# A hybrid encoder trunk on one core: the builder resumes its chains by an account of queues and tiles instead of by fixed times

## The chip, the core and the metric

The kernel runs on one core of one Trainium2 chip. The core has five engines with a queue of instructions each: TensorE (PE, matrix products; its weight loads are shown as PEld), VectorE (DVE), ScalarE (ACT), GpSimd (POOL) and SyncE (SP, which issues the DMAs). An engine takes its instructions in the order in which they stand in its queue and waits, where it must, on semaphores. The metric is the time of one execution on the device, in microseconds (us).

## The reference, cut to what matters

Two groups of tokens (512 of "prompt", 256 of "sample") go through the same two layers. They share the weights and nothing else.

```python
def swiglu(h, w_in, w_out):
    gate, up = jnp.split(h @ w_in, 2, axis=-1)
    return (jax.nn.silu(gate) * up) @ w_out

def mixer(h, lp, rope):
    z = h @ lp["w_mix_in"]
    xb, yb, zr, q, k, v = jnp.split(z, [...], axis=-1)
    o_lru = rglru_mixer(xb, yb, lp)          # conv, gates, scan in both directions
    o_rwkv = rwkv_mixer(zr, lp)              # 4 heads of 64, delta rule, both directions
    o_att = attention(q, k, v, ...)          # 6 heads, 2 of them for keys and values
    return jnp.concatenate([o_lru, o_rwkv, o_att], axis=-1) @ lp["w_mix_out"]

def layer(x, c, lp, rope):
    sh1, sc1, g1, ... = jnp.split(silu(c) @ lp["w_ada"] + lp["b_ada"], 9)
    h = rmsnorm(x, g[0]) * (1 + sc1) + sh1
    x = x + 0.5 * g1 * swiglu(h, ffn_w_in[0], ffn_w_out[0])
    h = rmsnorm(x, g[1]) * (1 + sc2) + sh2
    x = x + g2 * mixer(h, lp, rope)
    h = rmsnorm(x, g[2]) * (1 + sc3) + sh3
    return x + 0.5 * g3 * swiglu(h, ffn_w_in[1], ffn_w_out[1])
```

D_MODEL is 1024, D_FF 2816, DEPTH 2; all of it in float32.

## The kernel before

All activations are held transposed: features on the 128 partitions, tokens along the free axis. PS is the prompt sequence (512 columns), SS the sample sequence (256 columns).

**Dense products.** A float32 weight is loaded (`wr`), rounded to fp32r by ACT (`wh`, L270), and the rest is formed by DVE (`wl`, L271). An activation is split in the same way (`xn`, `an`, `xo`, each a pair). One product of a 128x128 block is three matmuls: wh by xh, wh by xl, wl by xh. The PSUM tiles name the stage: `pg`, `pu` (PS) and `pb` (SS) for the feed-forward input, `ops` for the feed-forward output and the mixer's output, `mip` for the mixer's input. These are 15,264 of the 21,882 matmuls. DVE and ACT have one `wl` and one `wh` to make for each 512 columns of weights; for SS, such a piece serves 12 matmuls of 256 columns, for PS 12 of 512.

**Chains.** Between them run small products that wait on each other through DVE, ACT and POOL. The rwkv chain of a pair of heads (`rwkv_pair`) is the longest: `up`/`ap` (gates), a scan on DVE (`cu`), `kkp` (norm of the key), `bp` (bonus), then `AR`, `csum`, `BK`, `aa` and `B` on DVE, POOL and ACT (L763 to L806), then `scps` (scores), `btps`, `vtps`, four levels of `yps`/`dps` (a triangular inverse), the loop `zps`/`saps`/`stps` over chunks, `ywp` (output), a group norm on DVE that ends in `yy` (L1011), `yp`, `gp`. It runs twice a layer for each sequence. Behind the second pair comes the mixer's output product, `ops<-xo`, whose inputs `xo` are split from tiles that were spilled (`ol`) and from `yy`. A norm is `ssp` (sum of squares), a reciprocal root in some 12 tiny DVE instructions, and eight pairs `xn` by DVE, ACT and every third by POOL.

**What sets the order.** PE's queue is written in exactly the order in which the builder emits (L1187, `manual_schedule`); the other engines are ordered by the framework's scheduler, which goes by the order of emission, with the weights' `wh` and `wl` put ahead (L268). The builder is a small planner (L57 to L100): threads are generators, `Sched.t` is the planned time of PE, and each matmul adds its cost to it. A thread that yields a number may go on when that much planned time has passed; the numbers are the table `LAT` (L44), one per step and sequence. PS and SS are "dense" threads; attention, lru and the rwkv pairs are spawned as small threads. When PS is in its chains, SS supplies dense work, and the other way round: the small threads go first unless PE's debt to the dense ones exceeds `SLACK`.

```python
LAT = {... 'CH': (0.96, 0.58), 'NRM': (3.0, 3.0), 'XO': (1.7, 4.0), 'PREP': (5.0, 8.2), ... 'R8': (8.64, 6.0)}
            th.ready = self.t + r        # a thread that yielded r
```

So the distance between two steps of a chain, counted in dense matmuls that stand between them in PE's queue, comes from this table alone.

Of the kernel before, what the change touches and what calls it, by code (L numbers as in the profile page):

```python
# [51 lines left out]
NR = 4  # L52

# [7 lines left out]
class Sched:  # L61
# [21 lines left out]

    def run(self):
        while self.threads:
            act = [th for th in self.threads if th.cond is None or th.cond()]
            assert act, "stuck"
            now = [th for th in act if th.ready <= self.t + 1e-9]
            if not now:
                self.t = min(th.ready for th in act)  # L90
                continue
            dn = sorted((th for th in now if th.dense), key=lambda h: (h.prio() if callable(h.prio) else h.prio, h.ready))
            sn = sorted((th for th in now if not th.dense), key=lambda h: (h.prio() if callable(h.prio) else h.prio, h.ready))
            t0 = self.t
            if sn and (self.debt <= SLACK or not dn):
                self.step(sn[0])
                self.debt += (self.t - t0) * self.ratio
            else:
                self.step(dn[0])
                self.debt = max(0.0, self.debt - (self.t - t0))  # L100

# [10 lines left out]
def trunk_kernel(ctx, tc, xT, cT, wadh, wada, wfi, wfo, wmi, wmo, prm, gatew, loraw, cst, rope, scanm, outT, dbg=None):  # L112
    nc = tc.nc
    V, A, G, PE = nc.vector, nc.scalar, nc.gpsimd, nc.tensor
    sch = Sched(RATIO)

# [13 lines left out]
    def dbank(n=512, name="db"):  # L130
        return psd.tile([128, n], F32, name=name, tag="d")

    def sbank(n=512, name="sb"):
        return pss.tile([128, n], F32, name=name, tag="m")
# [11 lines left out]

    def mm(out, lhsT, rhs, start=True, stop=True, cost=None):
        PE.matmul(out, lhsT, rhs, start=start, stop=stop, skip_group_check=True)  # L148
        k, m, n = lhsT.shape[0], lhsT.shape[-1], rhs.shape[-1]
        if cost is not None:  # L150
            sch.t += cost
        elif rhs.dtype == F32R:
            sch.t += (n / 2.4 if n >= 256 else 213) * 1e-3
        else:
            conc = 1.0
            if m <= 32:
                conc = 4.0
            elif m <= 64:
                conc = 2.0
            sch.t += max(4 * max(n, m) / 2.4 / conc, 33.0) * 1e-3  # L160

    def trp(out, src, idn, cost=0.11):
        PE.transpose(out, src, idn)
        sch.t += cost
# [47 lines left out]
    def ada_load(src):  # L212
        u = adap.tile([128, 1024], F32, name="adaw", tag="adaw")
        nc.sync.dma_start(out=u, in_=src)
        return [u[:, j * 256:j * 256 + 256] for j in range(4)]
# [21 lines left out]
    def ada(l, m, lat):  # L237
        ps = sbank(256, name="adaps")
        for k in range(KD):
            for j, u in enumerate(ada_load(wada[l * 9 + m, k])):  # L240
                mm(ps[32 * j:32 * j + 32, :], sc[:, k, :], u, start=(k == 0), stop=(k == KD - 1))
            if k % ADQ == ADQ - 1:
                yield lat
# [20 lines left out]
    def wtile(dt, name):  # L264
        return wsp.tile([128, 512], dt, name=name, tag=name)
# [30 lines left out]
    def weight_raw(u):  # L296
        raw = wsp.tile([128, 1024], F32, name="wr", tag="wr", bufs=NR)
        nc.sync.dma_start(out=raw[:, :u.shape[-1]], in_=u)
        return raw
# [85 lines left out]
    class Norm:  # L385
# [19 lines left out]
        def apply(self):  # L405
            q, l, i = self.q, self.l, self.i
            self.x = []
            for k in range(KD):
# [11 lines left out]
                yield LAT["CH"][q.i] if k < KD - 1 else LAT["NRM"][q.i]  # L420
# [99 lines left out]
    def mix_in(q, l, xs, M):  # L520
# [3 lines left out]
        nc.sync.dma_start(out=rp, in_=rope[:, :, 0:n])  # L524
# [70 lines left out]
    def attention(q, l, M):  # L595
        n, nt = q.n, q.nt
        yield lambda: M.stage >= 1
        yield LAT["A0"][q.i]
# [22 lines left out]
        yield LAT["A1"][q.i]  # L621
# [3 lines left out]
        def stA(u):  # L625
# [3 lines left out]
            mm(S, M.qs[j][b0:b0 + 64, c0:c0 + 128], kr[b0:b0 + 64, :])  # L629
# [22 lines left out]
        def stC(u):  # L652
# [6 lines left out]
            for kt in range(nt):  # L659
                mm(o[b0:b0 + 64, :], vt[:, kt * 128 + b0:kt * 128 + b0 + 64], PT[:, kt * 128:kt * 128 + 128],  # L660
                   start=(kt == 0), stop=(kt == nt - 1))
# [13 lines left out]
    def lru(q, l, M):  # L675
        p, d_, n = pr[l], prm_d[l], q.n
        yield lambda: M.stage >= 2
        yield LAT["L0"][q.i]
# [44 lines left out]
    def rwkv_pair(q, l, hp, M):  # L723
# [95 lines left out]
        for d in range(2):  # L819
            for h in range(2):  # L820
                SC[h][d] = c128(slot(q, "SC"))
            for c0 in range(0, nch, 4):
                pp = [sbank(512, name="scps") for h in range(2)]
                for c in range(4):
                    for h in range(2):
                        b = 64 * h
                        mm(pp[h][:, c * 128:c * 128 + 128], bk(h, d * nch + c0 + c), AR[d][b:b + 64, :, (c0 + c) * 64:(c0 + c) * 64 + 64],
                           cost=0.11)
# [13 lines left out]
        for e in range(nbk):  # L842
            pp = [sbank(wb, name="btps") for h in range(2)]
            for c in range(gpb):
                for h in range(2):
                    trp(ch(pp[h], c), bk(h, e * gpb + c), ident[64 * h:64 * h + 64, 64 * h:64 * h + 64], 0.03)
# [97 lines left out]
        for i in range(nch):  # L944
            gs = (i, NC2 - 1 - i)
            sel = slice(i, NC2 - i, NC2 - 1 - 2 * i)
            if i > 0:
                zp = sbank(128, name="zps")
                for d, g in enumerate(gs):
                    for b in (0, 64):  # L950
                        mm(zp[b:b + 64, d * 64:d * 64 + 64], ar(b, g, 0), S0[b:b + 64, g, :])
# [13 lines left out]
            for d, g in enumerate(gs):  # L965
                for h in range(2):
                    mm(dp[64 * h:64 * h + 64, d * 64:d * 64 + 64], ch(BT[h], g), ch(SAV[h], g))
# [66 lines left out]
    def layer_thread(q, th):  # L1034
# [5 lines left out]
        if not P0:  # L1040
            prio(-2)
            yield S0T
            for k in range(KD):
                nc.sync.dma_start(out=q.x[k], in_=xT[k][:, q.o:q.o + q.n])
# [8 lines left out]
        for l in range(DEPTH):  # L1053
# [45 lines left out]
            for k in range(4):  # L1099
                nc.sync.dma_start(out=q.xd[k], in_=q.xsp[l][k])  # L1100
# [178 lines left out]
```

## Time and profile before

| | |
|---|---|
| time, median of 3 runs | 3456.47 us (3454.62 to 3456.97) |
| the profiled execution | 3462.16 us, of which the span from first to last instruction 3459.2 us |
| mean granted clock of TensorE | 0.986 of full speed |
| busy share of the span | PE 97%, PEld 79%, DVE 58%, ACT 42%, POOL 15% |
| DMA queue of the loads | 441 MB, 40% of the 16 engines' span |

A busy PE is not a PE at its peak: matmuls overlap, so the distance from start to start is shorter than the duration shown, and a matmul at half clock counts as busy too. The stretches named later are: 674 to 1046 us and 2193 to 2524 us, where PS is in its rwkv chains and SS does dense work (layers 0 and 1); 1046 to 1184 us, where PS begins its second feed-forward; 2524 to 2816 us, the same in layer 1; 1184 to 1586 us, where SS is in its rwkv chains and PS does dense work.

### The profile page before, as it was taken

What the parts mean: (1) busy time and instruction counts of PE and PEld (TensorE: products, weight loads), DVE (VectorE), ACT (ScalarE), POOL (GpSimd) and SP (SyncE); (2) the same over time, 40 slices, a digit from 0 to 9 for tenths busy, and PEclk for the clock granted to TensorE, in tenths of its full rate; (3) what the DMA queues carried; (4) which work ended last, traced back from release to release, by engine and by line L of the source; (5) the groups of instructions that cost most, each with busy time, mean ns of one, the idle gap of its engine ahead of it and who ended that gap; (6) DMA issues with size and microseconds to landing.
All of it is one profiled execution on the core that took longest, in us unless ns stands there. A gap on an engine that the chain in (4) does not pass through costs nothing. (4 is left out here: it accounts for less than half of the span.)

```text
span 3459.2 us, 69173 instructions
## 1 busy us (share of the span) xinstructions
PE 3341.5 (97%) x28052; PEld 2734.0 (79%) x28052; DVE 2003.2 (58%) x3973; ACT 1448.2 (42%) x2730; POOL 512.1 (15%) x659
## 2 busy tenths in 40 slices
PE   7999999999899899999999999999899999999999
PEld 5777776678877777888888876788789978778899
DVE  4433365775776745546333476667557776446466
ACT  3322243644346433434333346534345564334354
POOL 1100020212221211111000111212211111111010
PEclk9999999999999999999999999999899999999999
DMA  7666674133342222423332331233245533223455
GB/s 276 219 206 208 203 270 145 57 104 113 100 153 93 83 80 83 132 90 119 92 98 86 119 114 62 79 110 102 82 161 164 179 106 108 63 91 125 138 177 161
DMA packets 151630, 445.80 MB, mean 129 GB/s; under 512 B 16912, under 2 KB 20752, under 8 KB 151312
## 3 DMA queue, kind: packets, MB, share of 16 engines
q1 hardware_dynamic: 151312, 441.39, 40.2%
q8 instruction: 220, 3.60, 0.4%
q14 instruction: 98, 0.80, 0.1%
HBM read 427.17 MB, written 14.16 MB: 128 GB/s over the span
## 5 line engine op out<-in xcount | busy, mean ns | idle before, releaser
L270 ACT ACTIVATE wh<-wr 128x512 fp32r<-128x512 f32 (+1 forms) x1368 | 816.6, 602 | 1572.1 <-PE ops L148 485.5
L271 DVE TENSOR_TENSOR wl<-wr,wh 128x512 fp32r<-128x512 f32 (+1 forms) x1368 | 907.3, 668 | 800.4 <-ACT wh L270 769.8
L148 PE MATMUL ops<-an,wh 128*128 128x512 f32 (+1 forms) x2816 | 717.8, 345 | 19.3 <-ACT an L351 7.3
L148 PEld LDWEIGHTS ops<-an,wh 128*128 128x128 f32 x2816 | 480.1, 190 | 99.1 <-issue 13.5
L148 PE MATMUL pb<-xn,wh 128*128 128x256 f32 x2816 | 525.1, 287 | 0.5 <-issue 0.5
L148 PE MATMUL ops<-an,wl 128*128 128x512 f32 (+1 forms) x1408 | 477.2, 339 | 0.1
L148 PE MATMUL pg<-xn,wh 128*128 128x512 f32 x1408 | 449.5, 400 | 7.8 <-ACT xn L417 5.9
L148 PEld LDWEIGHTS pb<-xn,wh 128*128 128x128 f32 x2816 | 433.6, 189 | 19.2 <-issue 11.2
L148 PE MATMUL pu<-xn,wh 128*128 128x512 f32 x1408 | 447.4, 399 | 0.0
L352 POOL TENSOR_TENSOR an<-sg,an 128x512 fp32r<-128x512 f32 (+1 forms) x176 | 192.3, 1093 | 1674.0 <-ACT an L351 1613.0
L148 PE MATMUL pb<-xn,wl 128*128 128x256 f32 x1408 | 396.4, 282 | 4.8 <-DVE wl L271 3.8
L431 DVE SCALAR_TENSOR_TENSOR x<-ops,gat,x 128x256 f32<-128x256 f32 (+1 forms) x352 | 215.8, 614 | 196.0 <-PE ops L148 190.6
L148 PE MATMUL mip<-xn,wh 128*128 128x512 f32 (+1 forms) x1216 | 314.2, 348 | 9.3 <-DVE f L583 2.9
L148 PEld LDWEIGHTS pg<-xn,wh 128*128 128x128 f32 x1408 | 260.1, 188 | 75.6 <-ACT xn L417 6.5
L148 PEld LDWEIGHTS pu<-xn,wh 128*128 128x128 f32 x1408 | 260.1, 188 | 65.5 <-issue 6.6
L148 PEld LDWEIGHTS ops<-an,wl 128*128 128x128 f32 x1408 | 267.0, 190 | 31.6 <-DVE wl L271 0.3
L148 PE MATMUL pg<-xn,wl 128*128 128x512 f32 x704 | 277.4, 394 | 0.0
L148 PE MATMUL pu<-xn,wl 128*128 128x512 f32 x704 | 276.8, 393 | 0.0
L148 PEld LDWEIGHTS pb<-xn,wl 128*128 128x128 f32 x1408 | 265.9, 189 | 6.0 <-DVE wl L271 4.8
L148 PEld LDWEIGHTS mip<-xn,wh 128*128 128x128 f32 x1216 | 208.2, 192 | 48.9 <-issue 12.3
L148 PE MATMUL mip<-xn,wl 128*128 128x512 f32 (+1 forms) x608 | 207.2, 341 | 0.0
L148 PEld LDWEIGHTS pg<-xn,wl 128*128 128x128 f32 x704 | 132.9, 189 | 30.7
(257 smaller groups left out, 3738.5 us busy)
## 6 DMA issues: line engine op xcount, KB each, us to landing
wr<-in_wfi_dram SPq DMA_DIRECT2D x352, 512.0 KB, 3.6
adaw<-in_wada_dram SPq DMA_DIRECT2D x128, 512.0 KB, 4.4
wr<-in_wfo_dram SPq DMA_DIRECT2D x192, 256.0 KB, 2.7
wr<-in_wfo_dram SPq DMA_DIRECT2D x128, 320.0 KB, 2.9
wr<-in_wmi_dram SPq DMA_DIRECT2D x76, 512.0 KB, 3.6
wr<-in_wmo_dram SPq DMA_DIRECT2D x32, 512.0 KB, 3.5
adaw<-in_wadh_dram SPq DMA_DIRECT2D x32, 256.0 KB, 5.2
xsp<-x SPq DMA_DIRECT2D x8, 512.0 KB, 3.6
```

What stands on the lines that cost most here:

```text
L148: PE.matmul(out, lhsT, rhs, start=start, stop=stop, skip_group_check=True)
L270: A.activation(out=hi[:, :n], in_=raw, func=AF.Copy)
L271: V.tensor_tensor(out=lo[:, :n], in0=raw, in1=hi[:, :n].bitcast(F32), op=ALU.subtract)
L352: eng.tensor_tensor(out=lo, in0=src, in1=hi.bitcast(F32), op=ALU.subtract)
L431: V.scalar_tensor_tensor(out=q.x[m], in0=ps, scalar=gat[l][:, i, m, q.i:q.i + 1], in1=q.x[m], op0=ALU.mult, op1=ALU.add)
```

## The change

An account (`Model`) is kept beside the planner. `Engine` wraps VectorE, ScalarE and GpSimd: each instruction still goes out as before, and the account books it on a list of busy intervals of that engine, in the first gap that is long enough from the moment on at which its inputs are ready, whether or not something later was already booked. Durations are linear in the size, with constants for kinds of instruction. For each tile the account keeps when it is written (`w`), read for the last time (`r`) and, for tiles that are taken through `alloc` (PSUM, weights, adaLN weights), when its buffer comes free (`free`). A tile of the slot pools isn't taken through `alloc`, so its `free` is 0, and a load into it (`load`) is booked as there at `DMAT` = 3.4 us from the start of the program. That an instruction writes a tile which an earlier one still reads isn't booked.

With it, a step resumes as follows. A chain that yields a positive `LAT` resumes 0.05 us after the last of the instructions that its step issued (`step_last`), so the numbers in `LAT` act as a flag; a yield of 0.0 is as before. Dense steps yield `At(...)`, the time at which the account has their weights and the next two activation pairs ready. Norms and the split of `xo` yield `At(step_last - 1.6)`. A small thread also waits until the account has one of the four PSUM buffers free. Planned costs of matmuls are raised (0.4531 ns a column for fp32r instead of 0.4167), and a change between dense and small matmuls costs 0.1 us in the plan. Instructions of every kind are as many as before: PE 21,882 matmuls, DVE 3,967 rows, ACT 2,660, POOL 664, SP 1,051.

```diff
+SWITCH = 0.1
+DMAT = 3.4
...
     def step(self, th):
+        self.mo.step_last = 0.0
...
+        elif isinstance(r, At):
+            th.ready = r.t
+        elif r > 0 and self.mo.step_last > 0:
+            th.ready = self.mo.step_last + 0.05
         else:
             th.ready = self.t + r
...
-            now = [th for th in act if th.ready <= self.t + 1e-9]
+            bank = self.mo.bank("m")
+            now = [th for th in act if max(th.ready, 0.0 if th.dense else bank) <= self.t + 1e-9]
...
+    def place(self, t0, dur):
+        iv = self.iv
+        k = len(iv)
+        while k > 0 and iv[k - 1][1] > t0:
+            k -= 1
+        s = t0
+        while k < len(iv) and iv[k][0] < s + dur:
+            s = max(s, iv[k][1])
+            k += 1
+        iv.insert(k, (s, s + dur))
...
+    def op(self, e, name, outs, ins, kw):
...
+        t0 = self.ready(*ins)
+        for a in outs:
+            t0 = max(t0, self.free.get(self.keys(a)[0][0], 0.0))
...
+        t = e.place(t0 + 0.06, d) + lag
+        for a in outs:
+            for k in self.keys(a):
+                self.w[k] = max(self.w.get(k, 0.0), t) if name != "memset" else max(self.w.get(k, 0.0), t)
...
+        self.step_last = max(self.step_last, t)
...
+    def dma(self, out, src):
+        t = max(self.free.get(self.keys(out)[0][0], 0.0), self.ready(src) if hasattr(src, "tensor") else 0.0)
+        for k in self.keys(out):
+            self.w[k] = t + DMAT
...
     def mm3(out, q, xs, every):
         nk = len(xs)
         for k, (xh, xl) in enumerate(xs):
             if k % 4 == 0:
+                wfill(q, look(q) + 1)
+                yield At(mo.ready(*q.wq[0], *xs[k], *xs[min(k + 1, nk - 1)]) if k else
+                         max(mo.ready(*q.wq[0], *xs[0], *xs[min(1, nk - 1)]), mo.free.get(out.tensor.name if hasattr(out, "tensor") else out.name, 0.0)))
                 wh, wl = wget(q)
+            elif k % every == 0:
+                yield At(mo.ready(*xs[k], *xs[min(k + 1, nk - 1)]))
...
-            if k % every == every - 1:
-                yield 0.0
...
                 self.x.append((xh, xl))
-                yield LAT["CH"][q.i] if k < KD - 1 else LAT["NRM"][q.i]
+                yield At(mo.step_last - 1.6)
...
             for k in range(3):
                 od.append(slot(q, "ol"))
-                nc.sync.dma_start(out=od[k], in_=q.osp[l][k])
+                load(od[k], q.osp[l][k])
             for t in [od[k // 2][:, k % 2, :] for k in range(6)] + M.orw:
                 xh, xl = pair(q, "xo")
                 split(xh, xl, t)
                 xo.append((xh, xl))
-                yield LAT["CH"][q.i]
+                yield At(mo.step_last - 1.6)
             M = None
             n3 = Norm(q, l, 2)
-            yield LAT["XO"][q.i]
             yield from out_proj(q, l, 1, xo, n3, EV[q.i])
```

Three places show what this does to the order. The first is PE's queue in SS's first rwkv pair of layer 0, from `kkp` to the first `scps`. Before:

```order
L148 MATMUL kkp<-ksq,cs 128x256
L148 MATMUL pu<-xn,wh 128x512 x2
L148 MATMUL pu<-xn,wl 128x512
...
L148 MATMUL bp<-kb,cs 128x256
L148 MATMUL pu<-xn,wh 128x512 x2
...
L148 MATMUL scps<-AR,BK 128x128
```

And now, in the same place:

```order
L309 MATMUL kkp<-ksq,cs 128x256
L309 MATMUL pu<-xn,wh 128x512 x2
L309 MATMUL pu<-xn,wl 128x512
...
L309 MATMUL bp<-kb,cs 128x256
L309 MATMUL pg<-xn,wh 128x512 x2
...
L309 MATMUL scps<-AR,BK 128x128
```

Before, 6 dense matmuls of 512 columns stand between `kkp` and `bp` and 96 between `bp` and `scps`, 102 in all. Now they are 24 and 18, 42 in all.

The second is PE's queue at the end of PS's second rwkv pair of layer 0, from the last output products `ywp` to the mixer's output product `ops<-xo`. Before:

```order
L148 MATMUL ywp<-S_10243,AR 64x64 x28
L148 MATMUL mip<-xn,wh 128x256 x2
...
L148 MATMUL yp<-cs,yy 64x64 x16
L148 MATMUL gp<-f,lw 128x512
L148 MATMUL mip<-xn,wh 128x256 x2
...
L148 MATMUL ops<-xo,wh 128x512 x2
L148 MATMUL ops<-xo,wl 128x512
```

And now:

```order
L309 MATMUL ywp<-S_10179,AR 64x64 x28
L309 MATMUL ssp<-acc,cs 128x256
L309 MATMUL yp<-cs,yy 64x64 x16
L309 MATMUL gp<-f,lw 128x512
L309 MATMUL ops<-xo,wh 128x512 x2
L309 MATMUL ops<-xo,wl 128x512
```

Before, 48 matmuls of SS stand between `ywp` and `yp` and 114 between `gp` and `ops<-xo`. Now there is one small `ssp` in the first gap and nothing in the second.

The third is DVE's queue behind the same `gp`, where `yy<-yy,gp` closes the pair and the eight low parts `xo` follow. Before:

```order
L1022 TENSOR_TENSOR yy<-yy,gp 128x512
L271 TENSOR_TENSOR wl<-wr,wh 128x512 x2
L352 TENSOR_TENSOR xo<-ol,xo 128x512 x2
L534 TENSOR_SCALAR qg<-mip,pr_99 128x256
L352 TENSOR_TENSOR xo<-ol,xo 128x512 x2
...
L352 TENSOR_TENSOR xo<-yy,xo 128x512 x2
```

And now:

```order
L128 TENSOR_TENSOR yy<-yy,gp 128x512
L128 SCALAR_TENSOR_TENSOR nx<-x_111,scl_132,rB 128x256
L128 SCALAR_TENSOR_TENSOR nx<-x_112,scl_132,rB 128x256
L128 TENSOR_TENSOR xo<-ol,xo 128x512 x2
L128 SCALAR_TENSOR_TENSOR xn<-nx,mod_130,xn 128x256 x2
L128 TENSOR_TENSOR xo<-ol,xo 128x512 x4
L128 TENSOR_TENSOR xo<-yy,xo 128x512
L128 TENSOR_TENSOR wl<-wr,wh 128x512
L128 TENSOR_TENSOR xo<-yy,xo 128x512
```

The eight splits now stand closer together, with five instructions of other work among them and ahead of them; they still stand behind `yy<-yy,gp`. (All wrapped instructions now carry line 128.)

## Rows read from the trace of the kernel before

**Rows 1.** The page: its first line.
```profile
span 3459.2 us, 69173 instructions
```

**Rows 2.** Windows: length; busy (instructions) of PE, PEld, DVE, ACT, POOL; clock; DMA; GB/s.
```profile
674.00:1046.00 372.00, 342.30 (x5092) 301.71 (x5091) 252.79 (x538) 156.09 (x308) 78.60 (x106) 0.96 0.37 114
1046.00:1184.00 138.00, 126.19 (x682) 98.74 (x681) 96.44 (x208) 83.65 (x171) 31.58 (x51) 0.95 0.30 95
1184.00:1586.00 402.00, 401.23 (x3284) 321.07 (x3284) 203.57 (x408) 139.69 (x264) 54.17 (x67) 1.00 0.31 95
2193.00:2524.00 331.00, 301.13 (x4799) 265.12 (x4799) 207.10 (x432) 136.13 (x268) 70.72 (x95) 0.94 0.31 94
2524.00:2816.00 292.00, 285.11 (x2083) 265.11 (x2082) 210.04 (x426) 157.32 (x301) 41.24 (x53) 0.99 0.53 168
```

**Rows 3.** Waits of PE: who waited for whom, us in total, times, longest.
```profile
PE scps L148 <- DVE BK L793: 13.8, 3, 6.1
...
PE pg L148 <- ACT xn L417: 5.9, 2, 5.5
...
PE yp L148 <- DVE yy L1011: 3.5, 3, 1.2
...
PE S L148 <- DVE qr L613: 2.3, 2, 1.4
```

**Rows 4.** Timeline of PE, PS's first rwkv pair: start, length, instruction, count [idle before].
```profile
710.67 0.40 PE L148 MATMUL ops<-an,wh 128*128 128x256 f32 x2
...
711.03 1.02 PE L148 MATMUL kkp<-ksq,cs 128*128 128x512 f32 x2
...
739.38 0.79 PE L148 MATMUL scps<-AR,BK 64*128 64x128 f32 x2 [6.06 <-DVE BK L793]
```

**Rows 5.** Timelines of DVE and ACT, the same pair: the last inputs of scps.
```profile
738.64 1.28 DVE L793 TENSOR_TENSOR BK<-aa,cu 128x512 f32<-128x512 f32 x2
...
739.36 2.00 ACT L806 ACTIVATE B<-BK 64x1024 f32<-64x1024 f32 x2 [4.24 <-DVE BK L793]
```

**Rows 6.** Timeline of PE, SS's first rwkv pair of layer 0.
```profile
1162.11 0.62 PE L148 MATMUL pu<-xn,wh 128*128 128x512 f32 x2
...
1162.80 0.59 PE L148 MATMUL kkp<-ksq,cs 128*128 128x256 f32 x2
...
1187.06 0.40 PE L148 MATMUL pu<-xn,wl 128*128 128x512 f32 x1
1187.38 0.37 PE L148 MATMUL scps<-AR,BK 64*128 64x128 f32 x1
```

**Rows 7.** Timelines of DVE and ACT, the same pair: the last inputs of scps.
```profile
1175.60 0.76 DVE L793 TENSOR_TENSOR BK<-aa,cu 128x256 f32<-128x256 f32 x2 [0.59 <-POOL aa L790]
...
1176.06 0.63 ACT L806 ACTIVATE B<-BK 64x512 f32<-64x512 f32 x1 [2.97 <-DVE BK L793]
```

**Rows 8.** Timeline of PE, end of PS's second rwkv pair of layer 0.
```profile
997.86 1.85 PE L148 MATMUL ywp<-S,AR 64*64 64x64 f32 x56
...
1013.55 1.15 PE L148 MATMUL yp<-cs,yy 64*64 64x64 f32 x32 [1.16 <-DVE yy L1011]
1014.63 1.12 PE L148 MATMUL gp<-f,lw 128*128 128x512 f32 x2
...
1029.01 0.64 PE L148 MATMUL ops<-xo,wh 128*128 128x512 f32 x2
```

**Rows 9.** Timeline of DVE, the same place.
```profile
1012.72 0.69 DVE L1011 TENSOR_TENSOR yy<-yy,rs 128x512 f32<-128x512 f32 x1
...
1019.77 1.29 DVE L352 TENSOR_TENSOR xo<-ol,xo 128x512 fp32r<-128x512 f32 x2
...
1028.90 1.28 DVE L352 TENSOR_TENSOR xo<-yy,xo 128x512 fp32r<-128x512 f32 x2
```

**Rows 10.** Timeline of PE: first use of PS's norm, layer 0.
```profile
1135.93 0.79 PE L148 MATMUL pg<-xn,wh 128*128 128x512 f32 x1 [5.45 <-ACT xn L417]
```

**Rows 11.** Windows around that wait (columns as in rows 2).
```profile
1133.00:1148.00 15.00, 8.73 (x34) 7.21 (x35) 14.89 (x21) 8.60 (x15) 5.83 (x13) 0.54 0.13 44
```

More of the change, by code (lines that the diff above doesn't have):

```diff
@@ L52, with __init__ @@
 NR = 4
+SWITCH = 0.1
+DMAT = 3.4
+class At:
+    def __init__(self, t):
+        self.t = t
 class Thread:
@@ L87, in run @@
             assert act, "stuck"
-            now = [th for th in act if th.ready <= self.t + 1e-9]
+            bank = self.mo.bank("m")
+            now = [th for th in act if max(th.ready, 0.0 if th.dense else bank) <= self.t + 1e-9]
             if not now:
-                self.t = min(th.ready for th in act)
+                self.t = min(max(th.ready, 0.0 if th.dense else bank) for th in act)
                 continue
@@ L100, in run, with __init__, __getattr__ @@
                 self.debt = max(0.0, self.debt - (self.t - t0))
+class Engine:
+    def __init__(self, real, m, kind):
+        self.real, self.m, self.kind, self.iv = real, m, kind, []
+    def __getattr__(self, name):
+        call = getattr(self.real, name)
+        def run(*args, **kw):
+            r = call(*args, **kw)
+            aps = [a for a in args if hasattr(a, "dtype") and hasattr(a, "shape")]
+            outs = [kw[k] for k in ("out", "accum_out") if kw.get(k) is not None]
+            ins = [v for k, v in kw.items() if k not in ("out", "accum_out") and hasattr(v, "dtype") and hasattr(v, "shape")]
+            if "out" not in kw:
+                outs, aps = outs + aps[:1], aps[1:]
+            self.m.op(self, name, outs, ins + aps, kw)
+            return r
+        return run
+    def place(self, t0, dur):
[8 more added lines that the diff above has]
+        iv.insert(k, (s, s + dur))
+        if len(iv) > 400:
+            del iv[:200]
+        return s + dur
@@ L149, in mm @@
         k, m, n = lhsT.shape[0], lhsT.shape[-1], rhs.shape[-1]
[L150 to L160, printed above, removed]
+        old = cost if cost is not None else (n / 2.4 if n >= 256 else 213) * 1e-3 if rhs.dtype == F32R else max(
+            4 * max(n, m) / 2.4 / (4 if m <= 32 else 2 if m <= 64 else 1), 33.0) * 1e-3
+        if cost is None:
+            if rhs.dtype == F32R:
+                cost = (n * 0.4531 if n >= 256 else 213) * 1e-3
+            else:
+                conc = 1.0
+                if m <= 32:
+                    conc = 4.0
+                elif m <= 64:
+                    conc = 2.0
+                cost = max(4 * max(n, m) * 0.4453 / conc, 33.0) * 1e-3
+        mo.mm(out, (lhsT, rhs), cost, old)
     def trp(out, src, idn, cost=0.11):
         PE.transpose(out, src, idn)
-        sch.t += cost
+        mo.mm(out, (src, idn), cost, cost)
     cs = const.tile([128, NCST], F32, name="cs")
@@ L597, in attention @@
         yield lambda: M.stage >= 1
-        yield LAT["A0"][q.i]
+        yield At(mo.ready(*M.sq))
         rps = sbank(3 * nt * 2, name="rqps")
@@ L620, in attention @@
         M.sq = M.vf = None
-        yield LAT["A1"][q.i]
+        yield At(mo.ready(kr, vt, *M.qs[0:3]))
         units = [(j, qt, hh) for j in range(3) for qt in range(nt) for hh in range(2)]
@@ L628, in stA @@
             S = sbank(n, name="S")
-            mm(S, M.qs[j][b0:b0 + 64, c0:c0 + 128], kr[b0:b0 + 64, :])
+            mm(S, M.qs[j][b0:b0 + 64, c0:c0 + 128], kr[b0:b0 + 64, :], cost=n * 2.1e-3)
             mx = tn(1, name="mx")
@@ L660, in stC @@
                 mm(o[b0:b0 + 64, :], vt[:, kt * 128 + b0:kt * 128 + b0 + 64], PT[:, kt * 128:kt * 128 + 128],
-                   start=(kt == 0), stop=(kt == nt - 1))
+                   start=(kt == 0), stop=(kt == nt - 1), cost=0.25)
             if hh == 1:
@@ L677, in lru @@
         yield lambda: M.stage >= 2
-        yield LAT["L0"][q.i]
+        yield At(mo.ready(*M.xc))
         M.ol = []
```

116 lines of the change are left out of this document (100 added, 16 removed).

## The prediction

> **What bounds the kernel now.** I read the page first, then the windows by stage, then PE's waits, and then the timelines around the waits that the change moves. The page gives a span of 3459.2 us [rows 1]; the profiled execution took 3462.16 us, 3.0 more, and 5.7 more than the median of the runs (3456.47). My sum is made on 3462.16, and 5.7 comes off at its end. PE is busy for 97% of the span, no other engine for more than 58%, so PE's queue is the bound, and only two things can be won or lost: time in which PE waits, and time in which it runs at half clock behind a wait.
>
> The windows show where these lie [rows 2]. While SS is in its chains (1184 to 1586 us) PE idles 402.00 - 401.23 = 0.8 us at clock 1.00: the order of before hides these chains entirely, and nothing is to be won there. While PS is in its chains PE idles 372.00 - 342.30 = 29.7 us at clock 0.96, and 29.9 us at 0.94 in layer 1. At the start of PS's second feed-forward (1046 to 1184) it idles 11.8 us at 0.95, in layer 1 (2524 to 2816) 6.9 us at 0.99. The half clock does not come by itself: in the 15 us around PE's wait of 5.45 us for `xn` [rows 10] the granted clock is 0.54 [rows 11], so 6.9 us of work are lost there besides the wait.
>
> Among PE's waits, `scps` for `BK` is 13.8 us in three, `pg` for `xn` 5.9, `yp` for `yy` 3.5, the attention's `S` for `qr` 2.3 [rows 3]. The question for each step is how long it takes on DVE, ACT and POOL, and how many dense matmuls stand beside it on PE. A dense matmul counts for its distance from the next start. With 256 columns three take 711.03 - 710.67 = 0.36 us, 0.12 each [rows 4]; with 512 columns 1162.80 - 1162.11 = 0.69, 0.23 each [rows 6].
>
> **SS, kkp to scps.** Before, 102 dense matmuls cover this step, 23.7 us; the rows agree (1162.80 to 1187.38) [rows 6]. It needs less: `kkp` ends at 1163.39, the last `B` is ready at 1176.69, 13.3 us later [rows 6, 7]. Of the 42 matmuls that now stand there (36 in the fourth pair) 9.7 us of cover are left (8.4), with `bp` 10.1 (8.8). So `scps` comes 3.2 us late in three pairs and 4.5 in one, 14 in all. The 13.3 us hold some dense work of DVE that the shorter step carries less of, so I take +12. Bounds: 0, if the chain shrinks with its cover, and 26, if each wait is followed by as much loss in clock as in rows 11. Matmuls taken from here stand elsewhere in the queue, where, by rows 2, nothing waits for them.
>
> **PS, kkp to scps.** Here `BK` already comes late: `kkp` starts at 711.03, `BK` ends at 739.92, PE waits 6.06 us [rows 4, 5]. From `lr` to `scps` the four pairs lose 3, 30, 15 and 30 matmuls of cover, 78 x 0.118 = 9.2 us. DVE is busy for 253 of the stretch's 372 us [rows 2] and the amount of other work in this part of its queue is nearly the same, so a good part of that shows as wait: +5 (0 to 9).
>
> **PS, ywp to yp.** The group norm takes 13.7 us from the end of `ywp` (999.71) to the last `yy` (1013.41) [rows 8, 9], and `yp` still waits 1.16 us behind its 48 matmuls in that pair. Over the four pairs the cover falls from 318 to 183 matmuls, by 16 us, to none in the second pair. Part of the 13.7 us is DVE doing other work, of which there is less now: +5 (0 to 16).
>
> **The split of xo.** Before, the first `xo` is ready at about 1020.4, 4.7 us after `gp` (1015.75), the last at 1030.18, 14.4 after it [rows 8, 9]; 114 matmuls, 13.4 us, lie between, and `ops` starts at 1029.01 with no wait. Now nothing lies between in layer 0 and 21 matmuls in layer 1 (138 before). The splits follow each other at 0.645 us [rows 9], with few instructions of other work among them, so the last should be there some 10 us after `gp`. PE would use it 7 x 0.7 = 4.9 us after it starts. That is 5 us of wait for PS in layer 0, 2.4 in layer 1, and for SS, where 12 and 6 matmuls of 0.23 us are left of 72, about 1 each: +9 (0 to 24, the latter if all the cover that was removed shows).
>
> **Norms.** These gain. PS's norms get more cover: from `ssp` to `pg` 54, 18 and 65 us of other PE work, where 5.7 to 13.5 stood. In 1046 to 1184 the 11.8 us of wait and 138 x 0.05 = 6.9 of clock make 18.7, most of it from this wait: -14. In 2524 to 2816 and SS's first `mip` -5, the other norms -3: -22 (-28 to -8).
>
> **The rest.** The wait of `S` for `qr` gets cover: -2.3 [rows 3]. A change between dense and small matmuls on PE costs 0.32 us where a dense start follows at 0.23 [rows 6], so 0.09; there are 997 such changes instead of 937: +5. Instructions, loads and bytes stay as they are. DVE's, ACT's and POOL's queues are ordered otherwise, without an added instruction, and outside these places PE's work covers them: 0. What SP's queue costs when loads are issued in another order no row shows; weight loads take 40% of the DMA engines and are ahead by several tiles, so 0 (-2 to 6).
>
> The sum is 12 + 5 + 5 + 9 - 22 - 2.3 + 5 = +12: 3474 us by the profiled execution, 5.7 less for the median, 3468 us.
>
> **Rivals.** The first is faster. It says that the covers which the old order kept were filled with their own delay: the weights' `wl` of the dense matmuls stand in DVE's queue among the chain's instructions, and when the matmuls leave, the chain shortens with them. Then only a third of the first four terms is left (+10), the norms give their 22, with attention 24, the changes cost 2 to 5: -12, 3444 us. For it speaks that `BK` waited only 0.59 us for POOL [rows 7] and was otherwise held by DVE's own queue. Against it: in the `xo` split and the group norm of PS DVE's instructions depend on each other and on `gp`, however little else is queued.
>
> The second is slower than my forecast. Each of the some 14 new waits would be followed by a stretch at half clock as in rows 11, costing 3 to 7 us apiece instead of the wait alone: +40 to +60 on the sum before the norms' gains, some 3500 us. For it: in PS's stretches clock 0.96 and 0.94 [rows 2] mean 15 and 20 us lost beside 30 of waits. [...] Against it: the waits in SS's chains stand between runs of dense matmuls.
>
> The Trainium skill's "TensorE: Matmul & The Clock Gate", Part 1, has the rule that "the default state is throttled, and activity releases the throttle." The trace agrees as far as it goes (0.54 behind the wait, [rows 11]). By that rule each new gap puts its price twice, which is this second rival.
>
> The third is that the change does not do what it says for time: chains, norms and dense steps get other positions, but gains and losses cancel, because PE has the same matmuls and 97% of the span is theirs: 3450 to 3462 us.
>
> **How the numbers follow.** My forecast has 0.38, with a range of its own from 3452 to 3485 us by the bounds above. The faster rival has 0.33, the half clock 0.14, no change 0.15. A difference under 0.2% (6.9 us, 3449.6 to 3463.4) can't be told from none. Of my forecast 0.7 lies above that and 0.27 within it; of the faster rival 0.85 lies below and 0.15 within; no change is mostly within. So faster 0.32, same 0.25, slower 0.43. A range that holds the time 8 times in 10 must take in both signs: 3430 to 3500 us.
>
> **What would show it.** In the changed kernel's waits of PE, `scps` should wait for `BK` or `B` in the SS stretches, some 3 us each, where it waited for nothing; `yp` for `yy` more than 3.5 us in all; `ops` for `xo` some 5 us behind PS's second pair; `pg` for `xn` no longer 5.5 us, and `S` for `qr` no more. The idle time of PE while SS is in its chains should rise from 0.8 us to some 6 to 10 in each layer. If the granted clock there falls well under 1.00, the half clock is right. If these stretches stay without waits, the chain shrank with its cover, and I am wrong with the first and largest term; if 3452 us is undercut, the norms gave what they promised and the covers removed were not needed.

## The result and the profile after

| | before | after |
|---|---|---|
| time, median | 3456.72 us of 4 runs (3454.62 to 3459.76) | 3547.60 us of 4 runs (3545.96 to 3551.69) |
| ratio of the two, 95% interval | | 1.0264 (1.0246 to 1.0282) |
| profiled execution, its span | 3462.16 us, 3459.2 us | 3551.69 us, 3549.9 us |
| span without a busy PE | 3459.2 - 3341.5 = 118 us | 3549.9 - 3381.5 = 168 us |
| mean granted clock of TensorE | 0.986, so 48 us lost | 0.972, so 99 us lost |

The change costs 91 us. The page of the kernel after, its first line and the engines' busy time:

```profile
span 3549.9 us, 69165 instructions
## 1 busy us (share of the span) xinstructions
PE 3381.5 (95%) x28052; PEld 2758.1 (78%) x28052; DVE 2014.6 (57%) x3973; ACT 1438.7 (41%) x2730; POOL 514.1 (14%) x659
```

The instructions of PE are the same in number (28,052). The span is 91 us longer: PE idles 50.7 us more, and for the same matmuls it is busy 3381.5 - 3341.5 = 40.0 us longer. The clock gives 51 us less, so part of what it lost lies in the waits, where it costs nothing. PE's waits in the kernel after (who waited for whom, us in total, times, longest), to be read against [rows 3]:

```profile
PE scps L309 <- DVE BK L128: 49.7, 8, 10.4
...
PE yp L309 <- DVE yy L128: 12.8, 5, 4.0
PE avp L309 <- ACT PT L128: 11.6, 5, 4.5
PE yps L309 <- DVE X L128: 8.6, 8, 2.9
...
PE gps L309 <- ACT P L128: 6.4, 4, 4.3
...
PE yp L309 <- DVE sh L128: 5.8, 1, 5.8
...
PE S L309 <- ACT gr L128: 2.5, 1, 2.5
PE ops L309 <- ACT xo L128: 2.5, 1, 2.5
...
PE pg L309 <- POOL xn L128: 1.4, 1, 1.4
```

`scps` waits for `BK` eight times instead of three: 37.9 us in PS's four pairs, where before had 13.8, and 11.8 in SS's. `yp` waits 18.6 us instead of 3.5 (2.6 of it in SS), and `avp` and `gps`, the small products of attention and lru, for 18 us where before had 1.5. The long wait of `pg` for `xn` is gone. PS's `S` waits for `qr` no more; the 2.5 us of `S` are another wait, of SS's `S` at 1125 us. The stretches of [rows 2], cut in the kernel after at the same places of PE's work (length; busy of PE, PEld, DVE, ACT, POOL with instructions; clock; DMA share; GB/s):

```profile
685.00:1075.00 390.00, 344.46 (x4966) 294.79 (x4965) 241.51 (x486) 152.00 (x299) 76.54 (x98) 0.93 0.32 101
1075.00:1220.00 145.00, 129.28 (x935) 104.99 (x934) 113.60 (x270) 85.13 (x179) 29.98 (x55) 0.92 0.31 98
1220.00:1631.00 411.00, 406.69 (x3125) 325.22 (x3124) 200.42 (x394) 139.53 (x264) 52.72 (x66) 0.99 0.31 92
2244.00:2589.00 345.00, 301.97 (x4653) 260.24 (x4653) 210.12 (x434) 134.42 (x267) 70.42 (x96) 0.92 0.28 84
2589.00:2882.00 293.00, 285.69 (x2168) 263.19 (x2166) 207.17 (x427) 152.93 (x303) 42.58 (x52) 0.99 0.52 162
```

PS's rwkv stretches are 18 and 14 us longer and their clock is 0.93 and 0.92 instead of 0.96 and 0.94. The first stretch in which the norm was to gain (1075 to 1220) idles 15.7 us, more than the 11.8 before. While SS is in its chains PE now waits 4.3 us at clock 0.99, where it waited 0.8 at 1.00.

PE in PS's first rwkv pair after (start, length, [idle before]), which answers to [rows 4]; then SS's first pair, which answers to [rows 6]:

```profile
731.77 1.02 PE L309 MATMUL kkp<-ksq,cs 128*128 128x512 f32 x2
...
739.00 1.02 PE L309 MATMUL bp<-kb,cs 128*128 128x512 f32 x2
...
758.16 0.79 PE L309 MATMUL scps<-AR,BK 64*128 64x128 f32 x2 [10.37 <-DVE BK L128]
...
1191.68 0.59 PE L309 MATMUL kkp<-ksq,cs 128*128 128x256 f32 x2
...
1205.42 0.48 PE L309 MATMUL scps<-AR,BK 64*128 64x128 f32 x2 [2.97 <-DVE BK L128]
```

DVE in the 14 us ahead of PS's `scps`, in part:

```profile
749.87 1.28 DVE L128 TENSOR_TENSOR wl<-wr,wh 128x512 fp32r<-128x512 f32 x2
751.07 1.28 DVE L128 SCALAR_TENSOR_TENSOR BK<-csum,cu 128x512 f32<-128x512 f32 x2
752.28 0.68 DVE L128 TENSOR_TENSOR wl<-wr,wh 128x512 fp32r<-128x512 f32 x1
752.88 0.41 DVE L128 SCALAR_TENSOR_TENSOR sg<-sg,pb 128x256 f32<-128x256 f32 x1
753.21 0.80 DVE L128 TENSOR_SCALAR aa<-aa,kah,ka 128x1024 f32<-128x1024 f32 x1
753.93 0.41 DVE L128 TENSOR_TENSOR sg<-sg,pb 128x256 f32<-128x256 f32 x1
754.26 2.71 DVE L128 TENSOR_TENSOR wl<-wr,wh 128x512 fp32r<-128x512 f32 x1
756.90 1.81 DVE L128 TENSOR_TENSOR BK<-aa,cu 128x512 f32<-128x512 f32 x2
```

DVE does not wait here; between the chain's instructions stand the `wl` of SS's weights. The account has them at the wrong time. It gives a new `wh` or `wl` the buffer with the earliest last use, and the last use of a tile that was made and not yet read by a matmul is the moment at which it was made. So each new weight is booked right behind an unread one, and the bookings fall behind. In the builder's own planned time (no time of the chip) the `wl` issued at 695 us is booked at 397, and the one issued at 3295 us at 2073; the median over all 1,368 is 815 us behind. `wl` is 916 us of DVE's work and `wh` 814 of ACT's, and a chain sees next to none of it.

The granted clock around the wait of `scps`, windows as above:

```profile
740.00:758.00 18.00, 7.79 (x67) 7.59 (x65) 17.83 (x28) 5.24 (x11) 6.34 (x4) 0.78 0.43 135
758.00:772.00 14.00, 13.42 (x130) 11.51 (x132) 10.12 (x20) 4.93 (x9) 0.91 (x1) 0.79 0.09 23
```

In the second window, behind the wait, 0.21 x 14 = 2.9 us are lost to the clock, on top of the 10.37.

PS's second rwkv pair of layer 0 ends so in the kernel after, which answers to [rows 8, 9]: PE from `ywp` to `yp`, then the last `yy` on DVE:

```profile
1020.31 1.85 PE L309 MATMUL ywp<-S,AR 64*64 64x64 f32 x56
...
1028.56 1.97 PE L309 MATMUL yp<-cs,yy 64*64 64x64 f32 x32 [5.77 <-DVE sh L128]
...
1027.72 0.69 DVE L128 TENSOR_TENSOR yy<-yy,rs 128x512 f32<-128x512 f32 x1
```

### The profile page after: what moved, and what is told of

Read it like the earlier page. It is cut to its first block, busy times and chain, and to the rows that moved or that the text cites. A ratio compares the mean times of both kernels' runs of the same rounds, so it can differ in the third digit from the quotient of the medians.

```text
span 3549.9 us, 69165 instructions
## 1 busy us (share of the span) xinstructions
PE 3381.5 (95%) x28052; PEld 2758.1 (78%) x28052; DVE 2014.6 (57%) x3973; ACT 1438.7 (41%) x2730; POOL 514.1 (14%) x659
## 5 line engine op out<-in xcount | busy, mean ns | idle before, releaser
L309 PEld LDWEIGHTS pu<-xn,wl 128*128 128x128 f32 x704 | 133.0, 189 | 30.8
```

## Experiments

The cover of a step is the dense matmuls that stand beside it in PE's queue. Theory A: the chains' covers are too short, because the account lacks the dense work of DVE and ACT. Rival B: the account is short for other reasons. Rival C: the loss sits in the dense steps, norms, xo or the planned costs. Later came theory F: the tables of before fit one alignment of the two sequences (which step of PS stands beside which of SS), and any shift of it costs; theory G is that only the parts' own waits cost. "After" below is 3547.6 us; before was measured beside each run, at 3457.9 to 3460.4. Ratios are to before.

**e1_weights_now.** After, with the weights booked near the planned time:

```diff
+        if self.keys(outs[0])[0][0][:2] in ("wh", "wl"):
+            t0 = max(t0, self.sch.t - 2.0)
```

> The changed kernel, but the account books the weights' wh and wl no earlier than 2.0 us ahead of the planned time at which they are issued; in the changed kernel it books them up to 1265 us in the past, so that its DVE and ACT look free while a chain runs. Theory A (the chain steps are too short because this dense work is missing from the account): between kkp and scps of PS's four pairs stand 198, 276, 210 and 84 dense matmuls instead of 120, 114, 126 and 114, the scps waits for BK fall from 49.7 us to under 20, and the time from 3548 to under 3505 us. Rival B (the account is short for other reasons, such as durations, hops between engines or buffers not yet read): the waits for BK stay over 35 us in all and the time within 15 us of 3548.

Measured 3523.97 us, ratio 1.0190 (1.0175 to 1.0206). Waits of PE:

```profile
PE yp L311 <- DVE yy L128: 16.5, 6, 6.5
PE scps L311 <- DVE BK L128: 15.7, 4, 5.8
PE ops L311 <- ACT an L128: 8.7, 3, 5.4
```

The waits for `BK` fall from 49.7 to 15.7 us as theory A has it, so it is the weights' bookings that made that step short. But the time falls by 24 us of the 91 and not by the 43 expected: PS's chains now take up to 276 dense matmuls from SS in one step, and SS's chain starts where none are left (`lr` to `kkp` without one dense matmul in layer 0).

**e2_table_chains.** After, with chains by the table:

```diff
-            th.ready = self.mo.step_last + 0.05
+            th.ready = self.t + r
```

> The changed kernel, but a chain that yields a number goes on after that planned time, as before; dense steps, norms, the xo split and the first two steps of attention and lru stay with the account. Theory A (the loss sits in the chains' resumption): 3460 to 3480 us, PE's waits for BK 10 to 20 us, for PT and P in attention and lru under 3. Rival C (the loss sits in the dense steps, norms or xo, or in the added changes between dense and small matmuls): over 3520 us.

Measured 3496.75 us, 1.0117 (1.0098 to 1.0137): between the two. 51 us are the chains', 39 are left for the rest, so C holds in part. Attention still waits:

```profile
PE avp L309 <- ACT PT L128: 13.4, 7, 3.8
PE ptp L326 <- DVE P L128: 12.0, 8, 3.2
```

**e5_prep_table.** After, with the table only for the yields OP, R1, PREP and R0 (`lr` to `scps`):

```diff
+        elif isinstance(r, Tab):
+            th.ready = self.t + r.r
...
-        yield LAT["PREP"][q.i]
+        yield Tab(LAT["PREP"][q.i])
...
```

> The changed kernel, with the rwkv steps from lr to scps alone resumed by the table again (159, 156, 144 and 156 dense matmuls from kkp to scps of PS, 90 to 105 of SS, as before). The scps waits for BK and B, 51 us, fall to about 15. If a wait costs its own length, the time falls by some 35 us to 3512; if a wait costs about twice its length, because TensorE runs at half clock behind it, it falls by 55 to 70 us to 3478 to 3492. If the loss sits elsewhere (group norm, attention, xo), by under 20.

Measured 3501.60 us, 1.0126 (1.0107 to 1.0145). `scps` waits for `BK` 14.4 us; 35 us of wait less, 46 us of time less. PE's idle time falls by 30 us (168 to 138), the clock rises to 0.979. Read as the price of these waits, that is more than their length and less than double; but the edit shifts the rest of the order too, and a shift alone can cost 20 us (c_slack below), so the price is not shown by it.

**e4_before_prep0.** Before, with PREP of PS at 0:

```diff
-LAT = {... 'PREP': (5.0, 8.2), ...}
+LAT = {... 'PREP': (0.0, 8.2), ...}
```

> The kernel before with one number changed: PREP of PS from 5.0 to 0.0, so that 48 dense matmuls fewer (51 in one pair), 195 in all or 23 us, stand ahead of scps in its four pairs. If a wait costs its own length: scps waits rise from 13.8 to about 35 us and the time by about 20 to 3477. If the half clock doubles it: +38 to +46 us, 3495 to 3503, and the mean granted clock falls from 0.986 to about 0.98. If the chain shrinks with its cover: within 10 us of 3457.

Measured 3475.97 us, 1.0048 (1.0033 to 1.0063), clock 0.982.

```profile
PE scps L148 <- DVE BK L793: 29.1, 4, 10.5
```

23 us of cover less, 15 us of this wait more (10 of all PE's idle time), 18 us of time more. Of the three expectations the first is nearest.

**The parts one by one.** The next kernels take after's code with every part undone, which issues PE's matmuls exactly in the order of before, and put one part back; their diffs are against that kernel, with "..." for what is left out.

**p_chain.** The chains by the account:

```diff
-        elif r > 0 and self.mo.step_last > 0:
-            th.ready = self.t + r
+        elif r > 0 and self.mo.step_last > 0 and not th.dense:
+            th.ready = self.mo.step_last + 0.05
```

> The order of the kernel before with one part of the change alone: chains that yield a number resume by the account (step_last + 0.05); planned costs, dense steps, norms, xo and the first steps of attention and lru as before. From kkp to scps stand 138, 144, 135 and 114 dense matmuls in PS's pairs (150, 168, 171, 168 before) and 48 in SS's (102). If the chains' resumption carries most of the loss (theory A): 3505 to 3520 us, PE waits for BK over 35 us. If it carries only what its own waits cost because the rest of the account is off: 3470 to 3490.

Measured 3510.05 us, 1.0154 (1.0140 to 1.0167): 51 us, more than half of the loss, as A says, though `BK` is waited for 25.0 us and not 35.

```profile
PE scps L309 <- DVE BK L128: 25.0, 6, 8.5
```

**p_cost.** The planned costs:

```diff
-        mo.mm(out, (lhsT, rhs), old, old)
+        mo.mm(out, (lhsT, rhs), cost, old)
-SWITCH = 0.0
+SWITCH = 0.1
-            bank = 0.0
+            bank = self.mo.bank("m")
...
-            pass
+            t = need
```

The last lines belong to the change too, though its description does not name them: a matmul whose inputs or PSUM buffer the account has ready only later moves the planned time up to that moment.

> The order of the kernel before with one part of the change alone: the planned costs (0.4531 ns a column, the small products' own, 0.1 us for each change between dense and small, and the wait for a PSUM buffer), with every yield by the table. The table's times then pass with fewer dense matmuls beside them (150, 150, 162, 150 from kkp to scps of PS). Rival C (the raised costs shorten every cover that the table gives, attention's above all): 3470 to 3485 us, waits for PT and P in attention 15 us or more. If the costs do nothing: within 5 us of 3457.

Measured 3499.86 us, 1.0117 (1.0103 to 1.0131), more than expected.

```profile
PE ptp L326 <- DVE P L128: 9.3, 6, 3.3
...
PE avp L309 <- ACT PT L128: 7.6, 4, 2.8
```

A table of planned times is worth less cover once the plan counts more for each matmul, and attention, whose steps had 12 or 18 matmuls beside them, shows it first. PE's waits rise by 16 us in all (3497.4 - 3363.7 = 134 for 118), its busy time by 22; 41 us of time come of it.

**p_xo.** The split of xo:

```diff
-                yield LAT["CH"][q.i]
+                yield At(mo.step_last - 1.6)
...
-            yield LAT["XO"][q.i]
```

> The order of the kernel before with one part of the change alone: the split of xo resumes by the account and the yield ahead of the mixer's output product is gone, so 30, 6, 30 and 6 dense matmuls stand between gp and ops instead of 114, 72, 138 and 72. The prediction's term: +9 us (0 to 24), PE waiting for xo some 3 to 5 us in each PS pair. With half clock behind the waits: +15 to +20.

Measured 3453.08 us, 0.9984 (0.9975 to 0.9993): faster than both kernels, against the forecast. PE at the place of [rows 8]:

```profile
1016.62 1.12 PE L309 MATMUL gp<-f,lw 128*128 128x512 f32 x2
...
1021.67 0.50 PE L309 MATMUL ops<-xo,wh 128*128 128x512 f32 x1 [0.41 <-ACT xo L128]
...
1022.51 0.50 PE L309 MATMUL ops<-xo,wh 128*128 128x512 f32 x1 [0.33 <-DVE xo L128]
```

`ops` starts 3.9 us after `gp` and waits 0.7 us in all, behind 30 matmuls where the kernel after has none. DVE makes a low part in 0.62 us, PE uses a pair in 0.70, so only the first pair matters. In the kernel after, with no cover at all, `ops` waits 3.2 us for `xo` there.

**p_first.** The first steps of attention and lru:

```diff
-        yield LAT["A0"][q.i]
+        yield At(mo.ready(*M.sq))
...
```

> The order of the kernel before with one part of the change alone: the first steps of attention (A0, A1) and of lru (L0) resume when the account has their inputs. The prediction said -2.3 us, since S waited for qr before. If the account is too early here as in the chains: +5 to +12 us, with waits of S, avp and gps.

Measured 3463.81 us, 1.0014 (1.0005 to 1.0023): 5 us slower.

```profile
1028.57 0.70 PE L309 MATMUL S<-qr 64*128 64x256 f32 x2 [2.10 <-DVE qr L128]
```

PS's two waits of `S` for `qr` (1.45 and 0.84 us before) are gone, but SS's `S`, with 256 columns, now waits 2.10 us. Where the 5 us come from is not shown.

**p_norm.** The norms:

```diff
-                yield LAT["CH"][q.i] if k < KD - 1 else LAT["NRM"][q.i]
+                yield At(mo.step_last - 1.6)
```

> The order of the kernel before with one part of the change alone: the eight steps of a norm resume 1.6 us ahead of the account's time instead of after the fixed CH and NRM. The prediction's term: -22 us (-28 to -8), 3435 us, pg no longer waiting 5.5 us for xn, clock loss at 1133 us gone. Rival: another wait of the same stretch takes its place and at most 5 us come off.

Measured 3479.96 us, 1.0067 (1.0055 to 1.0080): 21 us slower, where 22 were forecast to be won. PE in the stretch of [rows 10]:

```profile
1148.71 0.80 PE L309 MATMUL mip<-xn,wh 128*128 128x256 f32 x2 [5.26 <-DVE f L128]
...
1165.10 0.79 PE L309 MATMUL up<-f,lw 64*128 64x256 f32 x1 [4.73 <-ACT f L128]
```

`pg` no longer waits, but SS's `mip` and `up` wait for `f` in the same stretch, 5.3 and 4.7 us where the trace of before has 2.9 and 1.2: DVE and ACT work on PS's norm there, and whoever comes second waits. The rival has it for this place. The longest waits that are new lie elsewhere:

```profile
PE ops L309 <- ACT an L128: 17.6, 6, 6.9
```

SS's feed-forward now comes to the end of a group of `an` while PS's chain has DVE full, 17.6 us against 7.3 in the kernel before. On the other hand `scps` waits 6.0 us for `BK` instead of 13.8. PE's idle time rises by 10 us in all, so the 21 us are traced to single steps only in part.

**p_dense.** The dense steps:

```diff
-            if k % every == every - 1:
-                yield 0.0
...
+            elif k % every == 0:
+                yield At(mo.ready(*xs[k], *xs[min(k + 1, nk - 1)]))
...
```

> The order of the kernel before with one part of the change alone: the dense steps yield the account's time at which weights and activations are ready, instead of going on at once. Since the account has the weights ready hundreds of us early, it holds back for activations alone: within 7 us of 3457. If the finer stops inside a product break up runs of dense matmuls: +10 us and more changes between dense and small.

Measured 3474.77 us, 1.0051 (1.0038 to 1.0063): 16 us slower. Changes between dense and small matmuls hardly rise (947 for 935), so broken runs are not the reason. One long wait is new: `yp` in PS's second pair of layer 0 waits 5.4 us, because no dense matmul stands behind the last `ywp` there any more (48 before). What else makes the 16 us is open.

**p_scale.** p_cost with the raised costs alone:

```diff
-SWITCH = 0.1
+SWITCH = 0.0
-            bank = self.mo.bank("m")
+            bank = 0.0
...
-            t = need
+            pass
```

> As p_cost, but without the 0.1 us for a change between dense and small, without the wait for a PSUM buffer and without the planned wait of a matmul for its inputs: only the raised costs are left. From kkp to scps stand 150, 168, 171, 168 matmuls in PS as before. If the raised costs make p_cost's +41 us: 3490 to 3500 us. If the cost of a change and the PSUM wait make it: 3457 to 3470.

Measured 3487.27 us, 1.0086 (1.0072 to 1.0100): 28.5 of p_cost's 41 us, between the two expectations, although PS's steps from `kkp` to `scps` have their cover back. Little of it is waiting: PE idles 3486.3 - 3363.8 = 122 us, 5 more than in the kernel before, and is busy 22 us longer, at a granted clock of 0.981 (in c_s0t63, whose order is nearly that of before, the busy time differs by 6 us).

**p_xonorm.** p_xo and p_norm together (both diffs above).

> The order of the kernel before with the two parts of the change that may gain: xo (3453 us alone) and norms. If both terms stand side by side and the norms give what was predicted: 3430 us. If the norms give nothing: 3453 us. Slower than 3458 if the two collide behind PS's second pair, where the norm of SS and the split of xo share DVE.

Measured 3476.14 us, 1.0056 (1.0042 to 1.0069): slower than p_xo by 23 us; the norms take back what xo gives, `ops` waits for `an` 17.6 us as in p_norm.

**c_s0t63.** Before, with S0T 63 instead of 60.

> The kernel before with one number changed that belongs to no part of the change: S0T from 60 to 63, so SS starts 3 planned us later; every step between chains keeps its count of dense matmuls, only a few dense pieces change places early. Theory F (the tables of before fit one alignment of the two sequences, and any shift of it costs 10 to 25 us): the later stages coincide again with before, so within 5 us of 3458. Theory G (only the parts' own waits cost): also within 5 us. This run says how far a small shift that is made good later matters: over 10 us would speak for F strongly.

Measured 3459.20 us, 0.9997 (0.9988 to 1.0007): no difference. The shift is made good before the first chain, so this run does not tell F from G.

**c_slack.** Before, with one number that belongs to no part:

```diff
-SLACK = 0.6
+SLACK = 0.7
```

> The kernel before with one number changed that belongs to no part of the change: SLACK from 0.6 to 0.7, which lets small threads run ahead a little more and shifts the two sequences against each other through the whole program (869 changes between dense and small matmuls instead of 935, the table's covers kept). Theory F (any shift of the alignment costs): 3470 to 3485 us, with ops waiting for an or chains' steps waiting in new places. Theory G (only what the account's parts do harms): 3450 to 3462 us.

Measured 3480.18 us, 1.0056 (1.0041 to 1.0071): 20 us slower, as F has it.

```profile
PE dps L148 <- issue: 15.4, 12, 2.2
...
PE ops L148 <- DVE sg L455: 8.9, 4, 6.2
PE mip L148 <- ACT xn L417: 8.9, 1, 8.9
PE avp L148 <- ACT PT L649: 8.5, 3, 5.7
```

("issue": the profile shows nothing that PE waited for.) A shift alone costs about what p_norm and p_dense cost, by waits in steps whose table this run leaves as it was.

**p_chain_max.** p_chain, but never shorter than the table:

```diff
-            th.ready = self.mo.step_last + 0.05
+            th.ready = max(self.t + r, self.mo.step_last + 0.05)
```

> As p_chain, but a chain resumes at the later of the account's time and the table's, so no cover is shorter than before (kkp to scps of PS 216, 162, 210, 228 instead of 138, 144, 135, 114). If the short covers make p_chain's +51 us: 3455 to 3470, waits for BK under 5. If the shift of alignment makes it: 3485 or more, with the waits in other places (ops for an, dps, the start of SS's chain).

Measured 3477.14 us, 1.0049 (1.0031 to 1.0067): between the two.

```profile
PE scps L309 <- DVE BK L128: 1.6, 1, 1.6
```

So 34 of p_chain's 51 us go when the covers are kept, and 17 stay, about what a shift costs in c_slack. One cover is 6 matmuls shorter than in the kernel before all the same (162 for 168 in PS's second pair), and the others are up to 66 longer.

**e7_old_costs.** Dense steps, norms, xo and first steps together.

> The order of the kernel before with the account's four other parts together (dense steps, norms, xo, first steps of attention and lru), planned costs and chains as before. If the parts add up as measured alone (16 + 21 - 6 + 5): 3494 us. If each costs by throwing the alignment off once, the second and third do no more harm: 3470 to 3482. If their waits compound: over 3500.

Measured 3490.88 us, 1.0085 (1.0066 to 1.0104): 30 us, against 36 by the sum of the four measured alone. They add up nearly, though not by the same waits: the longest is one of 11.3 us of `yp` in PS's second pair.

## Why the prediction was wrong

The way was right, and the size was not: +12 us forecast, +91 measured, outside 3430 to 3500. Three terms of the sum failed most: the planned costs, priced at +5 by the changes between dense and small alone, give +41 (p_cost); the norms, -22, give +21 (p_norm); and PS's step from `kkp` to `scps`, +5, brings 24 us of wait. That the way came out right is partly luck, since the terms miss on both sides. By its own steps:

- **SS, kkp to scps: right.** 14 us of late `scps` were worked out, 3.2 in three pairs and 4.5 in one; they come 2.5 to 3.8 us late, 11.8 in all, and the waits while SS is in its chains rise from 0.8 to 4.3 us in layer 0. The need of 13.3 us from [rows 6, 7] was a good measure, because the dense work of DVE in it stayed.
- **PS, kkp to scps: the size, by a wrong place to count from.** I counted cover from `lr` (78 matmuls less) and took +5. What stands ahead of `kkp` covers nothing, since `kkp` waited for nobody before either; the work behind it is what PE waits for. From `kkp` the cover falls by 183 matmuls (150, 168, 171, 168 to 120, 114, 126, 114), 183 x 0.118 = 21.6 us. The waits of `scps` rise by 36 us with SS's, 24 of it in PS.
- **PS, ywp to yp: near the upper bound.** +12.5 us of wait in PS (15.9 for 3.5), where I took +5 of 0 to 16; SS's 2.6 were not counted. The 13.7 us of [rows 8, 9] were no need of the group norm: in the second pair, with no cover at all, it takes 6.2 us from the end of `ywp` (1022.16) to the last `yy` (1028.41), with little else in DVE's queue, and `yp` waits 5.8 of them. Here the first rival, by which a chain shrinks with its cover, was right. (The `sh` that the profile names belongs to SS's norm and begins 0.1 us before that `yy` ends.)
- **The split of xo: too large.** +9 forecast; in the kernel after `ops` waits 3.2 us for `xo`, in PS's layer 0 alone, and p_xo, which leaves 30 matmuls of cover there, gives -6. The 14.4 us to the last `xo` [rows 9] were no need of the splits: in the kernel before DVE has `wl`, `qg`, `rot` and `qr` between them.
- **Norms: wrong in sign.** -22 forecast, p_norm gives +21. The wait of `pg` went as forecast. That "most of" the stretch's 18.7 us came from this wait was the failing step: the stretch's other waits, `mip` and `up` for `f`, hung on the same DVE queue and grew. Where the rest of the 21 us lies is shown only in part.
- **The wait of S: as forecast, and no gain.** PS's two waits for `qr` are gone, but SS's `S` waits 2.5 us instead (the profile names ACT's `gr`), and p_first is 5 us slower.
- **What the sum lacked.** I priced the planned costs only by the 60 changes between dense and small (+5). p_cost gives +41. They shorten every cover that is given in planned time, and the later steps of attention and lru, which I did not count at all, wait 17 us more in the kernel after (`avp` and `gps`).
- **The half clock.** I gave 0.14 to the rival by which each wait is paid twice. In the kernel after the 91 us are 50.7 of more idle time and 40.0 of longer busy time, with 51 us more of clock lost; in e4_before_prep0 it was 15 of wait and 18 of time. So its mechanism was at work in the kernel as a whole, though the waits of e4_before_prep0 cost little more than themselves; which of the other waits cost more was not told apart. In p_scale nearly all of the loss is longer busy time. My own measure was too high: of the 6.9 us that I took from [rows 11], PE is busy for 8.73 of the 15 us only, so at most 0.46 x 8.73 = 4.0 cost time.
- **The third rival** (gains and losses cancel) had no gain to cancel with but xo's.

How the 91 us divide is shown only in part: the chains 51 us alone, some 34 of it by covers that are too short (p_chain against p_chain_max); the planned costs 41 alone; dense steps, norms, xo and first steps 30 together. That is more than 91, so they overlap. One reading, not shown, is that each holds the price of a shift, about 17 to 20 us, once. That a shift costs this much is shown by c_slack for one shift; that every shift does is not, and p_xo is one that does not cost.

## What to carry to other kernels

A planner that resumes steps by an account is as good as what it books: check first that the bookings keep up with the planned time, above all for prefetched work whose buffers it recycles. Count the cover of a wait from the last point at which the chain itself was held, and add every other step whose cover is given in the same unit when that unit changes. Before crediting an edit with a wait removed, look who else waits for the same engine in the same stretch, and run one control that shifts the order without the edit.

## What the runs showed of the hardware

DVE's `wl` of 128x512 takes 0.69 us (median of those that lie beside no work of POOL in the kernel after). When the first `wl` beside POOL's `aa` begins behind it, it ends only after POOL. POOL's row for the `wl` at 754.26 above is the first of these; the second is the `aa` of PS's last pair in the kernel before:

```profile
754.09 2.34 POOL L128 TENSOR_TENSOR aa<-aa,f 128x1024 f32<-128x1024 f32 x1 [5.83 <-DVE aa L128]
...
2404.03 3.32 POOL L790 TENSOR_TENSOR aa<-aa,f 128x1024 f32<-128x1024 f32 x1 [14.48 <-DVE aa L789]
```

DVE's 2.71 us end 0.54 after POOL's 2.34. In the kernel before, the `wl` that begin 0.2 us behind the `aa` of PS's pairs in layer 0 take 2.67 and 2.73 us. In its two pairs of layer 1 a `wl` begins first, and it is POOL's `aa` that becomes longer, 2.82 and 3.32 us. The Trainium skill says of the port that VectorE and GpSimd share that "it's an exclusive lock (not a bandwidth split)" ("Trainium Architecture — The Big Picture", What this means for kernel authors); this trace agrees: of an `aa` and the first `wl` beside it, the one that began second was the longer one (a second `wl` right behind such a first one goes ahead of POOL too and takes 0.69 us). The account books the `wl` at 0.61 us and knows nothing of it, and in the kernel before the two meet in each of PS's four pairs.
